# Windowed attention with split operands: the values' high and low halves in one 128-column stationary operand

## The chip, the cores and the metric

The kernel runs on one core of a Trainium2 chip, in float32 throughout. The metric is the device time of one launch in microseconds (us). The kernel before takes 1700.15 us, the median of three runs (1699.94, 1700.15 and 1702.44).

Engine names follow the profile: PE is TensorE's matmul stream and PEld its weight loads, which overlap it; DVE is VectorE, ACT is ScalarE, POOL is GpSimd, SP is the queue that issues most DMAs. PSUM is the accumulator memory into which PE writes.

## The reference

The reference is a two-layer transformer block for 512 tokens and 256 context tokens, width 1024. Layer 0 (even) mixes tokens by a gated MLP and a differential attention, layer 1 (odd) by a windowed attention with a sink; each layer ends with a SwiGLU feed-forward network (FFN) of hidden width 2816. Every matrix product must come out in float32 accuracy. The part that the change touches is the odd attention, cut to its core:

```python
def sink_attend(q, kvs, sink):            # 16 query heads, 4 key/value heads of 64
    for k, v, mask in kvs:                # a band of up to 3 blocks of 128 keys, and the 256 context keys
        s = einsum('bqhgd,bkhd->bhgqk', q, k) * ATTN_SCALE     # masked in the band
    p = softmax(concatenate(scores + [s_sink]))
    out = sum over kvs of einsum('bhgqk,bkhd->bqhgd', p, v)

def odd_mixer(...):
    q, k, v = split(h @ w_qkv, ...)       # rope on q and k
    o = lax.map(block, ...)               # 4 query blocks of 128
    y = o @ w_out
```

## The kernel before

**Arithmetic.** PE takes its operands in a rounded 32-bit format (fp32r). To keep float32 accuracy, a value is split in a high part (the rounded value, written by ACT) and a low part (the rest, a subtraction on DVE or POOL): `split` at L113 to L116 for activations, `unit` at L67 to L79 for weights. A product then takes three passes, high times high, high times low and low times high, which is the helper `mm3` at L95 to L101 (one line for each pass: L99, L100, L101).

**Layout.** Activations stand transposed, features on the 128 partitions and tokens along the free dimension. The order in which each engine meets its instructions is not written by hand: the code is recorded in program order, and a scheduler that estimates durations interleaves independent pieces; afterwards every engine runs its own list strictly in order. Tiles come from pools in which a tag has a fixed number of buffers; a new tile of a tag waits until its buffer's last reader is done. PSUM tags are `b` (three banks, `bank`, shown as `pb`), `f` (one bank, `fill`, `pf`) and `w` (two double banks, `wide`, `pw`).

**The odd attention** (`odd`, L1070 to L1241). Keys and values are projected first; the values of six blocks of 128 tokens are split by L115 and L116 into tiles `vhi` and `vlo` of 128 x 256 (four heads of 64). The work is then cut into two halves of 256 tokens and four key/value heads g; in `attend(g, half)` two query blocks i follow each other. One block does this:

1. `softmax`: for four query heads, scores by six or more matmuls into a `pw` bank (L1150, masks L1155, L1158), the row maximum (L1161) and a small minimum (L1162) on DVE, the exponential on ACT (L1164).
2. For each of the 4 or 5 key blocks kb (18 for the four query blocks, 72 in all): four transposes on PE into a bank `pt` (L1186), the split of that 128 x 512 tile (high on ACT, L115; low on DVE, L116), and `mm3` of the values with it into the block's accumulator `po`, the lower 64 partitions of a `b` bank. The stationary operand is `vhi` or `vlo` of one head, 128 x 64, the moving operand is 128 x 512.
3. Two ACT copies (L1194) bring the 64 x 512 accumulator to the output tile `raw`, whose partitions hold two heads each.
4. After two query blocks, four small transposes (L1201) and one DVE product (L1203) apply the softmax's denominators.

So `po`, `pt` and the bank of step 4 share the three `b` banks.

Other work is laid beside the attention: during the first half, the query projections of the next heads (`project_q`, into `pf`), and during the second half the output projection of the first half (`project(0, ...)`, 192 matmuls into `pf`), with its residual (L757), the squares of the new rows (L769 on ACT) and their sum (L773 on DVE). From that sum follow, still before the end of the attention, the reciprocal root (four matmuls L149 into `pf`, the small DVE steps L156 and L128 to L132, L165, and L175 on PE) and the FFN's modulated input of the first 256 tokens (L831 on DVE, L835 on ACT). After the attention comes the output projection of the second half (`project(1, ...)`, 192 matmuls into `pb`, whose weights' low parts are made on DVE, L78), then the same chain for the second 256 tokens, and the FFN.

The squares' tiles come from `tmp()` (L110): tag `q` of a pool that lives through the whole kernel, 128 x 512, two buffers, used in the program's order.

## Time and profile before

| what | value |
|---|---|
| median of three runs | 1700.15 us |
| profiled execution, its own time | 1697.54 us |
| its span on the chip | 1695.8 us |
| PE, DVE, ACT, POOL busy in the span | 92%, 68%, 44%, 48% |
| odd attention (first score matmul to last value matmul) | about 1039 to 1248 us of the span |
| output projection of the second half | 1247.9 to 1277.4 us |

The profiled execution lies 2.6 us under the median and 1.74 us over its own span. A busy share of PE counts each matmul from its start to the modelled end of its pipeline, so that neighbours overlap; the distance from one start to the next is what a matmul costs. In a list of groups, a row gives source line, engine, operation, output and input tiles, shapes, count, then busy time and mean duration, then idle time of the engine just before and what ended it. In a list of waits, a row says who waited for whom, how long in total, how often, and the longest. The chain of waits is followed back from the last instruction; the row "by line" gives the shares of a stretch.

### The profile page before, as it was taken

What the parts mean: (1) busy time and instruction counts of PE and PEld (TensorE: products, weight loads), DVE (VectorE), ACT (ScalarE), POOL (GpSimd) and SP (SyncE); (2) the same over time, 40 slices, a digit from 0 to 9 for tenths busy, and PEclk for the clock granted to TensorE, in tenths of its full rate; (3) what the DMA queues carried; (4) which work ended last, traced back from release to release, by engine and by line L of the source; (5) the groups of instructions that cost most, each with busy time, mean ns of one, the idle gap of its engine ahead of it and who ended that gap; (6) DMA issues with size and microseconds to landing.
All of it is one profiled execution on the core that took longest, in us unless ns stands there. A gap on an engine that the chain in (4) does not pass through costs nothing.

```text
span 1695.8 us, 24602 instructions
## 1 busy us (share of the span) xinstructions
PE 1558.7 (92%) x9415; PEld 1379.5 (81%) x9415; DVE 1145.4 (68%) x2037; ACT 752.8 (44%) x1521; POOL 806.8 (48%) x586
## 2 busy tenths in 40 slices
PE   6999989798899999999999988999987898999996
PEld 4776878698798889888899977778866788888986
DVE  4613788856967677666765676777769865756566
ACT  3413676433533233333333345676655444444443
POOL 0562211232675566656665336512115665666673
PEclk9999989899899899999999999999998999999998
DMA  8753100241032343344341112101140322222311
GB/s 312 290 184 133 32 1 1 87 159 41 25 125 88 124 136 110 127 136 135 132 132 38 49 63 75 51 7 45 50 146 10 125 90 98 87 100 78 110 38 50
DMA packets 47958, 161.98 MB, mean 96 GB/s; under 512 B 5472, under 2 KB 9952, under 8 KB 40160
## 3 DMA queue, kind: packets, MB, share of 16 engines
q1 hardware_dynamic: 47696, 160.28, 27.6%
q8 instruction: 74, 1.21, 0.3%
q14 instruction: 44, 0.36, 0.1%
q10 hardware_dynamic: 144, 0.13, 0.0%
HBM read 158.29 MB, written 2.10 MB: 95 GB/s over the span
## 4 chain that ended last, share of the span: by engine, by line
PE 65%; DVE 18%; DMA 6%; ACT 4%; issue 3%; POOL 3%; POOLq 0%; SPq 0%; DVEq 0%; ACTq 0%
PE pb L100 9%; PE pb L101 9%; PE pb L99 9%; PE pw L99 8%; PE pw L100 8%; PE pw L101 7%; DMA raw<-ffn_in 6%; POOL w L904 3%; DVE t L925 2%; PE pf L99 2%; PE pf L100 2%; PE pf L101 2%; PE pf L349 2%; DVE sq L925 1%; PE pb L1186 1%
## 5 line engine op out<-in xcount | busy, mean ns | idle before, releaser
L78 POOL TENSOR_TENSOR w<-raw,w 128x512 fp32r<-128x512 f32 (+1 forms) x84 | 128.6, 1540 | 234.3 <-ACT w L75 211.8
L99 PE MATMUL pw<-ax,w 128*128 128x384 f32 (+2 forms) x648 | 211.9, 331 | 18.0 <-DVE q L972 5.7
L904 POOL TENSOR_TENSOR w<-t,w 128x512 fp32r<-128x512 f32 x106 | 156.4, 1476 | 149.1 <-ACT w L901 146.0
L100 PE MATMUL pw<-ax,w 128*128 128x384 f32 (+2 forms) x648 | 210.7, 326 | 2.7 <-DVE ax L456 1.4
L101 PE MATMUL pw<-ax,w 128*128 128x384 f32 (+2 forms) x648 | 208.4, 324 | 3.1 <-DVE w L904 3.1
L757 DVE SCALAR_TENSOR_TENSOR xT<-pb,mod,xT 128x512 f32<-128x512 f32 (+3 forms) x208 | 143.9, 703 | 68.3 <-PE pb L101 67.9
L904 POOL TENSOR_TENSOR w<-raw,w 128x512 fp32r<-128x512 f32 x111 | 155.7, 1414 | 59.2 <-ACT w L901 59.2
L99 PE MATMUL pb<-hh,w 128*128 128x512 f32 x480 | 167.4, 363 | 14.8 <-ACT hh L115 7.9
L100 PE MATMUL pb<-hh,w 128*128 128x512 f32 x480 | 172.3, 361 | 0.7 <-POOL hh L116 0.2
L99 PE MATMUL pw<-T,w 128*128 128x384 f32 (+1 forms) x504 | 158.7, 318 | 12.2 <-DVE hs L968 9.5
L101 PE MATMUL pb<-hh,w 128*128 128x512 f32 x480 | 168.7, 359 | 0.0
L901 ACT CAST w<-t 128x512 fp32r<-128x512 f32 x120 | 74.2, 620 | 208.1 <-DVE t L925 176.8
L100 PE MATMUL pw<-T,w 128*128 128x384 f32 (+1 forms) x504 | 159.1, 316 | 7.0 <-DVE T L116 4.1
L101 PE MATMUL pw<-T,w 128*128 128x384 f32 (+1 forms) x504 | 158.3, 314 | 0.0
L99 PEld LDWEIGHTS pw<-ax,w 128*128 128x128 f32 x648 | 125.0, 194 | 32.8 <-DVE q L972 9.2
L100 PEld LDWEIGHTS pw<-ax,w 128*128 128x128 f32 x648 | 125.3, 193 | 10.5 <-DVE ax L193 3.3
L101 PEld LDWEIGHTS pw<-ax,w 128*128 128x128 f32 x648 | 124.8, 193 | 6.4 <-DVE w L904 3.3
L904 POOL TENSOR_TENSOR w<-rawo,w 128x512 fp32r<-128x512 f32 x74 | 107.2, 1448 | 39.1 <-ACT w L901 39.1
L99 PEld LDWEIGHTS pb<-hh,w 128*128 128x128 f32 x480 | 90.6, 191 | 28.5 <-ACT hh L115 9.0
L99 PEld LDWEIGHTS pw<-T,w 128*128 128x128 f32 x504 | 97.3, 194 | 18.9 <-DVE hs L968 11.9
L99 PE MATMUL pb<-ax,w 128*128 128x256 f32 (+1 forms) x344 | 106.8, 313 | 4.1 <-ACT w L75 2.2
L100 PE MATMUL pb<-ax,w 128*128 128x256 f32 (+1 forms) x344 | 106.3, 309 | 2.1 <-DVE ax L116 2.1
(381 smaller groups left out, 4324.4 us busy)
## 6 DMA issues: line engine op xcount, KB each, us to landing
raw<-ffn_in SPq DMA_DIRECT2D x44, 1024.0 KB, 5.7
ar<-ada SPq DMA_DIRECT2D x24, 1024.0 KB, 7.0
ar<-ada SPq DMA_DIRECT2D x48, 512.0 KB, 3.5
rawo<-ffn_out SPq DMA_DIRECT2D x44, 512.0 KB, 3.8
raw<-odd_out SPq DMA_DIRECT2D x32, 256.0 KB, 2.7
raw<-qk SPq DMA_DIRECT2D x16, 256.0 KB, 7.8
raw<-uv SPq DMA_DIRECT2D x16, 256.0 KB, 2.7
raw<-even_out SPq DMA_DIRECT2D x8, 512.0 KB, 3.5
```

What stands on the lines that cost most here:

```text
L78: eng.tensor_tensor(lo, raw, hi.bitcast(F32), ALU.subtract)
L99: mm(out, s[0], m[0], start=start, stop=False, **kw)
L100: mm(out, s[0], m[1], start=False, stop=False, **kw)
L101: mm(out, s[1], m[0], start=False, stop=stop, **kw)
L349: nc.tensor.matmul(ps[32 * q:32 * q + 32, :w], cst[:, k, :], t[:, w * q:w * q + w], start=k == 0, stop=k == KT - 1, skip_group_check=True)
L757: self.nc.vector.scalar_tensor_tensor(h, ps[:, r], self.modcol(l, j, m, who), h, ALU.mult, ALU.add)
L901: nc.scalar.copy(t[:, 0, :], src)
L904: eng.tensor_tensor(t[:, 1, :], src, t[:, 0, :].bitcast(F32), ALU.subtract)
L925: nc.vector.tensor_tensor(t, x, y, how)
L1186: nc.tensor.transpose(pt[:, x * P:(x + 1) * P], es[2 * (x % 2) + x // 2][:, kb * P:(kb + 1) * P], self.ident)
```

## The change

The values' high and low parts of one head become the two halves of one stationary operand of 128 columns. Against each of the two parts of the transposed probabilities it gives, in one pass, high values in the accumulator's partitions 0 to 63 and low values in partitions 64 to 127. So a key block takes two matmuls in place of three, and the product low times low, which was left out, is now in the sum. The accumulator `po` fills a whole bank. The two halves are joined at the end of each query block: ACT copies the half that lies in the other partitions to a `tmp()` tile (tag `q`), and DVE adds it to the half in PSUM into `raw`; two copies and two additions for each block, where two copies stood. The splits of the values and of the probabilities have the same number of instructions and elements; those of the values write runs of 64 elements into a tile that interleaves both parts by head.

```diff
-        vhi, vlo = [], []
+        V = []
...
         for tb in range(6):
-            hv, lv = [Rk.tile([P, TC], F32R, name=f"v1_{p}_{tb}") for p in range(2)]
-            self.split(hv, lv, acc[tb])
-            vhi.append(hv)
-            vlo.append(lv)
+            v = Rk.tile([P, 4, 2, 64], F32R, name=f"v1_{tb}")
+            self.split(v[:, :, 0, :], v[:, :, 1, :], acc[tb].rearrange("p (g d) -> p g d", d=64))
+            V.append(v.rearrange("p g c d -> p g (c d)"))
...
-                po = self.bank()[0:64, :]
+                po = self.bank()
...
-                    V = [v[vb][:, 64 * g:64 * g + 64] for v in (vhi, vlo)]
-                    self.mm3(po, V, (th, tl), kb == 0, kb == nb - 1)
+
+                    for p, t in enumerate((th, tl)):
+                        nc.tensor.matmul(po, V[vb][:, g, :], t, start=kb == 0 and p == 0, stop=kb == nb - 1 and p == 1)
+                c = slice(i % 2 * P, i % 2 * P + P)
+                o = raw[half, g]
                 pov = po.rearrange("p (h a q) -> p h a q", h=2, q=P)
+                lo = self.tmp()[:, :TC].rearrange("p (a q) -> p a q", q=P)
                 for par in range(2):
-                    nc.scalar.copy(raw[half, g][64 * par:64 * par + 64, :, i % 2 * P:i % 2 * P + P], pov[:, par, :, :])
+                    X = slice(64 * par, 64 * par + 64)
+                    nc.scalar.copy(lo[X], pov[64 - 64 * par:128 - 64 * par, par, :, :])
+                    nc.vector.tensor_tensor(o[X, :, c], pov[X, par, :, :], lo[X], ALU.add)
```

The scheduler sees other durations and other tiles and writes other lists. What differs beside the edits: the first half's seven sums of squares (L773), with the squares on ACT, the reciprocal root and the modulated input, which stood inside the attention, now stand after its last addition on DVE. On PE the projection of the second half is cut by them: 66 matmuls, the four L149, 30 matmuls, L175, 96 matmuls, where 192 stood in one piece. From the second L149 on, PE's list is the same as before.

## The prediction

> **What bounds the kernel now.** I read the page first, then busy time by stretch of the odd attention, then the chain of waits in each stretch. The page says that PE is the busiest engine; the span and PE's row:

> ```profile
> span 1695.8 us, 24602 instructions
> PE 1558.7 (92%) x9415; PEld 1379.5 (81%) x9415; DVE 1145.4 (68%) x2037; ACT 752.8 (44%) x1521; POOL 806.8 (48%) x586
> ```

> An average over stages says nothing about this one. Busy time in four stretches of the attention (columns: stretch, length, then PE, PEld, DVE, ACT, POOL busy with counts, granted clock, DMA share, GB/s):

> ```profile
> 1058.00:1098.00 40.00, 38.59 (x207) 31.24 (x208) 29.65 (x54) 23.01 (x49) 20.54 (x17) 1.00 0.17 53
> 1098.00:1158.00 60.00, 57.44 (x367) 45.24 (x365) 46.84 (x108) 43.94 (x108) 10.06 (x13) 1.00 0.03 10
> 1158.00:1208.00 50.00, 49.47 (x365) 44.69 (x366) 35.28 (x73) 34.22 (x83) 18.00 (x16) 1.00 0.23 69
> 1208.00:1248.00 40.00, 35.42 (x219) 26.17 (x219) 29.54 (x77) 25.24 (x61) 2.73 (x4) 1.00 0.19 67
> ```

> The first and the third have filling work on PE (query projections, then the output projection); the second and the fourth have nearly none. DVE is 74, 78, 71 and 74% busy. The value matmuls alone, in the same stretches (first pair after the length: PE busy and count):

> ```profile
> 1058.00:1098.00 40.00, 8.17 (x27) 3.51 (x27) 0.00 (x0) 0.00 (x0) 1.00 0.17 53
> 1098.00:1158.00 60.00, 26.98 (x81) 10.04 (x81) 0.00 (x0) 0.00 (x0) 1.00 0.03 10
> 1158.00:1208.00 50.00, 15.93 (x49) 6.20 (x49) 0.00 (x0) 0.00 (x0) 1.00 0.23 69
> 1208.00:1248.00 40.00, 20.02 (x59) 7.09 (x59) 0.00 (x0) 0.00 (x0) 1.00 0.19 67
> ```

> The chain of waits by line, one row for each stretch:

> ```profile
> by line: PE pf L99 14.6%; PE pf L101 13.2%; PE pf L100 13.1%; DVE sa L1161 6.0%; DVE sh L243 5.5%; DVE pt L116 5.0%; PE pb L1186 4.7%; DVE sa L1166 4.4%; DVE qf L244 4.3%; DVE sa L1162 3.9%; DVE qa L259 3.4%; PE pw L1150 3.3%; PE pw L1158 2
> by line: PE pb L1186 13.6%; PE pw L1150 12.7%; PE pb L100 9.2%; PE pw L1158 9.1%; PE pb L101 8.2%; DVE sa L1161 6.3%; PE pb L99 6.2%; ACT e L1164 6.0%; issue 5.0%; ACT pt L115 4.7%; DVE pt L116 4.5%; PE pw L1155 3.8%; ACT o L1194 3.7%; ACT
> by line: PE pb L1186 14.0%; PE pf L99 13.2%; PE pf L100 13.1%; PE pf L101 12.9%; PE pw L1150 9.1%; PE pb L100 7.8%; PE pw L1158 7.5%; PE pb L101 7.4%; PE pb L99 6.9%; PE pw L1155 3.2%; issue 1.5%; DVE pt L116 1.4%; ACT e L1164 1.1%; PE pb L
> by line: PE pb L1186 12.5%; PE pb L100 11.1%; DVE pt L116 10.2%; ACT pt L115 9.8%; PE pb L101 8.2%; ACT e L1164 7.2%; PE pw L1150 7.2%; PE pb L99 6.3%; PE pw L1158 5.8%; issue 3.8%; DVE sa L1161 3.5%; PE pw L1155 2.3%; DVE hm L831 1.9%; ACT
> ```

> In the third stretch the shares of PE shown add to 95%: PE is the limit there. In the second and fourth PE holds some 60%, and the rest goes round ACT and DVE: transposes, split on ACT, low part on DVE, matmul. Who waits for whom there:

> ```profile
> ACT pt L115 <- PE pb L1186: 28.6, 31, 2.6
> DVE pt L116 <- ACT pt L115: 21.4, 24, 3.1
> ACT o L1194 <- PE pb L101: 8.6, 9, 1.8
> PEld pb L100 <- DVE pt L116: 8.0, 16, 1.1
> PEld pb L99 <- ACT pt L115: 3.2, 6, 1.0
> ```

> **The change part by part.**

> *72 matmuls go.* What one costs is the distance between starts:

> ```profile
> 1133.22 0.40 PE L99 MATMUL pb<-pt,v 128*64 128x512 f32 x1
> 1133.45 0.39 PE L100 MATMUL pb<-pt,v 128*64 128x512 f32 x1
> 1133.68 0.39 PE L101 MATMUL pb<-pt,v 128*64 128x512 f32 x1
> 1133.91 0.27 PE L1186 MATMUL pb<-ident,e 128*128 128x128 f32 x1
> ```

> 0.23 us each, so 72 x 0.23 = 16.6 us of PE's list, one third of the counts above: 9, 27, 16 and 20 matmuls, or 2.1, 6.2, 3.7 and 4.6 us. What the chain gives of it: in the third stretch all of it, 3.7. In the second L101 holds 8.2% of 60 us = 4.9, in the fourth 8.2% of 40 = 3.3; there I count on a part, since DVE, which gets the additions, and the loop over ACT and DVE stand close behind: half of 4.9, 2.5, and 2.0 of 3.3. In the first stretch the rows of the query projection and its rope lead the chain and I take 1.0 of 2.1. Sum: 1.0 + 2.5 + 3.7 + 2.0 = 9.2 us. The ends: nothing but the third stretch (3.7), and everything that lies on the chain (2.1 + 4.9 + 3.7 + 3.3 = 14.0).

> *The remaining 144 have 128 columns of weights for 64.* Their nearest rows, a query projection of 128 columns and the old pass, differ little in matmul, more in weight load:

> ```profile
> L101 PE MATMUL pb<-pt,v 128*64 128x512 f32 x72 | 28.4, 395 | 0.0
> L101 PE MATMUL pf<-ax,w 128*128 128x512 f32 x49 | 19.2, 391 | 0.0
> L101 PEld LDWEIGHTS pb<-pt,v 128*64 128x64 f32 x72 | 9.7, 135 | 1.9
> L101 PEld LDWEIGHTS pf<-ax,w 128*128 128x128 f32 x112 | 21.1, 189 | 2.2
> ```

> A load of 189 ns hides under the 0.23 us of the matmul before it. Where a load waits itself (16 + 6 times in the list of waits) the 54 ns show: 22 x 0.054 = 1.2 us at most, 0.5 taken.

> *32 additions come on DVE, 64 x 256 from PSUM and SBUF.* Nearest rows: the low part of the values (128 x 256 out of PSUM), on ACT the copies of the same 64 x 256, which stay, and a subtraction of twice the length (weights' low parts, after the attention):

> ```profile
> L116 DVE TENSOR_TENSOR v<-pb,v x6: 411/414/424, 1023.2 to 1026.0; 128x256 fp32r<-128x256 f32 x6
> L1194 ACT COPY o<-pb x32: 352/366/368, 1077.9 to 1248.1; 64x256 f32<-64x256 f32 x32
> L78 DVE TENSOR_TENSOR w<-raw,w 128x512 fp32r<-128x512 f32 x11 | 7.2, 686 | 3.7 <-ACT w L75 3.6
> ```

> I take the 0.41 of the first row, which has as many elements along each partition: 32 x 0.41 = 13.1 us, ends 32 x 0.37 = 11.7 and 32 x 0.69 = 22.1. In the first and third stretch they lie beside PE's work. In the second they are 27 / 4.5 = 6 blocks x 0.82 = 4.9 us on a DVE that was busy for 46.8 of 60: that is why I left half of L101's chain time out there. In the fourth they are 4.4 x 0.82 = 3.6 us, and about as much leaves it (below).

> *po is held longer.* Its bank came free after two copies (0.73 us); now it waits for the second addition, and in DVE's new list a row maximum or a low part stands between the two additions of most blocks. At the 0.69 of a 128 x 512 subtraction that is 0.41 + 0.69 = 1.1 us later, 16 times, on one of three banks. The transposes of the next block's second key block wait for it. I cost it at nothing, because PE's list has one or two groups of score matmuls ahead of those transposes; without that cover it is 16 x 1.1 = 17.6 us, the first rival.

> *The copies on ACT, the splits of the values.* Same count and elements; nothing. Twelve splits with runs of 64 elements lie ahead of the first query projection, ends 0 and 12 x 0.2 = 2.4 us if each were half as long again.

> *The squares' chain moves behind the attention.* The new `tmp()` tiles are the last users of tag `q` in program order, so six of seven squares wait for the last additions. Behind them come the reciprocal root and the eight L831, into the projection of the second half. Its rows now, and what the later stage hangs on:

> ```profile
> 1247.86 0.36 PE L99 MATMUL pb<-ax,w 128*128 128x256 f32 x1
> 1261.02 0.41 PE L99 MATMUL pb<-ax,w 128*128 128x256 f32 x1
> 1261.23 0.41 PE L100 MATMUL pb<-ax,w 128*128 128x256 f32 x1
> 1276.88 0.28 PE L101 MATMUL pb<-ax,w 128*128 128x256 f32 x1
> 1277.00 0.28 PE L99 MATMUL pb<-ax,w 128*128 128x256 f32 x1
> 1277.36 0.60 PE L149 MATMUL pb<-ones,sq 128*128 128x128 f32 x4
> 1247.62 2.43 DVE L831 SCALAR_TENSOR_TENSOR hh<-xT,mod,pf 128x256 f32<-128x256 f32 x6
> L757 DVE SCALAR_TENSOR_TENSOR xT<-pb,mod,xT 128x256 f32<-128x256 f32 x6 | 2.9, 481 | 3.4 <-PE pb L101 3.4
> L773 DVE TENSOR_TENSOR sq<-sq,q 128x256 f32<-128x256 f32 x6 | 2.5, 420 | 1.6 <-ACT q L769 1.6
> by line: DVE t L925 18.8%; DVE ax L116 7.0%; DVE w L904 6.6%; DVE hh L873 6.0%; DVE sq L925 5.5%; DVE hm L873 5.0%; DVE sm L130 4.5%; DVE sm L131 4.5%; DVE hs L974 4.0%; DVE hh L831 3.4%; DVE hm L833 3.2%; DVE sm L132 2.6%; DVE T L116 2.3%;
> ```

> 192 matmuls at 0.12 are 23.0 us; they take 1277.36 - 1247.86 = 29.5, with 6.5 us of waits for weights and of slow matmuls. DVE is busy for 12.6 us of 1258 to 1278 (7.2 + 2.9 + 2.5), so there is room. In the new list: 66 matmuls, 7.9 us, in which DVE adds seven squares (2.9); L149, 0.5; 30 matmuls, 3.6, beside the root's small steps, which I take to be no longer than that; L175; then PE's last 96 wait for the ninth weight split, and ahead of it on DVE stand a residual, two sums, eight L831 and the split itself: 0.48 + 0.84 + 8 x 0.41 + 0.69 = 5.3 us idle; then 11.5. Sum 28.8, to which I add half of today's 6.5 of waits: 32.0, that is +2.5. Ends: -1.5 (what waits today is ready by then) and +6 (all 6.5 again). The last row says that DVE paces the start of the FFN, whose list is unchanged, so this goes through to the end.

> *Sum.* -9.2 + 0.5 + 2.5 = -6.2 us. Against the profiled execution's 1697.54 that is 1691.3; the median of the runs, 2.6 us above it, goes to 1693.9, say 1694.

> **The rivals.**

> *Slower: the accumulator's bank.* If PE has to wait for `po`'s second addition, the attention's blocks get longer by up to 1.1 us each. Two busy consumers speak for it: DVE, 78% busy in the second stretch, goes to (46.8 + 4.9) / 60 = 86% if the length stays. The cover by score matmuls speaks against it, and the old copies' wait, 8.6 us in 9 cases, was ACT's. It decides from 6.2 / 16 = 0.39 us a block; at 0.75 it is +12.0 - 6.2 = +5.8: 1706.

> *All of it.* If the loop over ACT and DVE has slack wherever L101 lay on the chain: -14.0 + 0.5 + 2.5 = -11.0: 1689. The third stretch's 95% speaks for it, the second's 60% against.

> *No change: the passes were not the limit.* If in the second and fourth stretch PE only waits longer for the loop over ACT and DVE (28.6 and 21.4 us of waits in the whole attention today), 3.7 + 1.0 is left, and with +4 at the joint it is 1700.15 - 0.7 = 1699.5.

> *A slower clock at the joint.* The matmuls at 1261.02 stand 0.21 apart, those at 1276.88 0.12: a stretch of PE at nearly half rate. One or two more such stretches of some 3.5 us, brought on by the 5.3 us in which PE would idle, cost 1.5 to 3 us, and give 1695.5 to 1697. [...] The two distances here, 0.21 and 0.12, agree with half against full.

> **How the numbers follow.** The sum as worked out 0.40 (own range 1690 to 1697), all of it 0.13, no change 0.13, the clock 0.08, the bank 0.26. About 0.2% (3.4 us) is what a measurement of this kernel can tell from no change. Faster: 0.40 + 0.13 = 0.53; same: 0.13 + 0.08 = 0.21; slower 0.26. The range takes the upper half of "all of it" and the lower half of the slower case: 1686 to 1706.

> **What would show it.** Right: 144 value matmuls with starts 0.23 apart; the stretch from the first score matmul to the last value matmul, 1039 to 1248 now, some 9 us shorter; 32 additions of about 0.4; one idle gap of 4 to 5 us in PE after L175; the second L149 some 32 us after the projection's first matmul. Wrong: waits of transposes (L1185 in the new numbering) for the additions (L1199), or DVE over 85% busy in the second stretch at the old length. The sum falls if the FFN's part, whose list is the same, moves by more than 2 us.

## The result, and the profile after

The changed kernel takes 1706.36 us (median of 5 executions, 1702.07 to 1709.53), the kernel before in its five 1700.15 (1699.74 to 1702.44): a ratio of 1.0038 with a 95% interval of 1.0022 to 1.0054. It is slower, by 6.5 us. 1694 was forecast, and the median lies 0.4 us above the range of 1686 to 1706.

The profiled execution took 1705.45 us. The page's span and engines (busy us, share, instructions):

```profile
span 1703.7 us, 24513 instructions
PE 1551.6 (91%) x9343; PEld 1375.5 (81%) x9343; DVE 1151.5 (68%) x2069; ACT 754.6 (44%) x1521; POOL 809.3 (48%) x586
```

72 matmuls are gone and PE is busy for 7.1 us less than before; the program is longer all the same. The same four stretches of the attention as in the prediction, all engines, then the value matmuls alone in the second and the third:

```profile
1058.00:1098.00 40.00, 38.01 (x205) 31.69 (x205) 30.79 (x58) 23.61 (x50) 21.36 (x18) 1.00 0.17 53
1098.00:1158.00 60.00, 50.68 (x311) 41.53 (x311) 48.25 (x111) 41.01 (x99) 9.19 (x12) 0.97 0.03 10
1158.00:1208.00 50.00, 46.88 (x348) 43.20 (x347) 34.01 (x72) 31.75 (x73) 16.90 (x15) 1.00 0.23 74
1208.00:1248.00 40.00, 33.73 (x202) 25.45 (x201) 31.53 (x76) 27.64 (x67) 2.92 (x4) 1.00 0.16 61
```

```profile
1098.00:1158.00 60.00, 20.73 (x52) 9.28 (x52) 0.97 0.03 10
1158.00:1208.00 50.00, 12.03 (x31) 5.26 (x29) 1.00 0.23 74
```

PE, at 57.4 of 60 us before, now stands at 50.7 in the second stretch: it idles for 9.3 us there. DVE went from 46.8 to 48.3, 80% of the stretch: no engine is full. Who waits for whom, from the first query projection to the last value matmul (waiting engine, tile and line, released by; us, times, longest):

```profile
PEld pb L1191 <- DVE pt L116: 15.1, 24, 1.6
PE pb L1191 <- DVE pt L116: 7.6, 18, 1.4
DVE o L1199 <- ACT q L1198: 4.0, 6, 1.4
PEld pb L1185 <- DVE o L1208: 2.8, 3, 1.2
PE pb L1185 <- DVE o L1208: 2.0, 3, 0.9
PE pb L1185 <- DVE o L1199: 0.3, 1, 0.3
PEld pb L1185 <- DVE o L1199: 0.3, 2, 0.2
```

The same view of the kernel before:

```profile
PEld pb L100 <- DVE pt L116: 8.0, 16, 1.1
PE pb L100 <- DVE pt L116: 2.5, 8, 0.9
PEld pb L1186 <- DVE o L1203: 0.4, 1, 0.4
```

The value pass that uses the low parts of the transposed probabilities (L116 on DVE) waits for them about twice as long as before: 22.7 us in its two rows together, 10.5 before. (The rows of PEld and of PE overlap in time, so such a sum counts waits and isn't lost time.) New are the waits of the transposes (L1185) for the product L1208, which comes after the last addition of a pair of blocks and holds a bank that they need. The waits for the additions themselves, which the first rival forecast, are 0.6 us.

Where the 7.9 us between the two profiled executions arose, in sections cut at PE's rows (start of the first query projection; last value matmul; second L149; end): -0.1 ahead of the attention, +3.6 in it (223.3 to 226.9), +2.8 at the joint (30.1 to 32.9), +1.5 in the FFN (418.4 to 419.9).

**Half-rate stretches.** Before these numbers are compared further, one thing has to be taken out of them. The first query projections of the kernel before, and of a kernel whose list is the same there (*x5_layout* below), one row for each matmul (start, us, engine, line; in brackets the idle time before it):

```profile
1032.12 0.47 PE L99 MATMUL pf<-ax,w 128*128 128x512 f32 x1 [2.49 <-DVE qf L244]
...
1033.56 0.63 PE L101 MATMUL pf<-ax,w 128*128 128x512 f32 x1
1033.98 0.63 PE L99 MATMUL pf<-ax,w 128*128 128x512 f32 x1
```

```profile
1035.09 0.47 PE L99 MATMUL pf<-ax,w 128*128 128x512 f32 x1 [2.49 <-DVE qf L244]
...
1036.32 0.39 PE L101 MATMUL pf<-ax,w 128*128 128x512 f32 x1
1036.55 0.40 PE L99 MATMUL pf<-ax,w 128*128 128x512 f32 x1
```

PE stood still for the same 2.49 us in both. Then the matmuls stand 0.42 us apart in one execution for some 3.4 us (granted clock 0.50 from 1033.1 to 1036.5 us), and 0.23 apart in the other (clock 1.00). That execution of the kernel before finishes its first block 2.5 us later (52.3 against 49.8 us from the projection's start), and from there on all blocks take the same time to 0.2 us. The attention of the changed kernel holds two such stretches, this one and another of 3.4 us around 1133:

```profile
1127.80:1131.20 3.40, 2.50 (x16) 1.79 (x14) 3.31 (x6) 1.33 (x3) 1.29 (x1) 1.00 0.14 40
1131.20:1134.60 3.40, 2.67 (x8) 2.01 (x9) 1.12 (x2) 2.66 (x7) 0.00 (x0) 0.62 0.10 37
```

A kernel with nearly the same order of work (*e2_own_tag*) has no such stretch at that place, and the block there is 1.3 us shorter. So below, next to the time, stands the length of the attention with such stretches taken out: 2.3 us for the one at the first projections (the difference of the two attentions above, 223.3 and 221.0), 1.3 for each further one. The first is measured on equal lists, the further ones cost 1.0 to 1.5 (*x6_prio* below); carried over to other kernels both are estimates.

### The profile page after: what moved, and what is told of

It is laid out like the page before. It is cut to its first block, busy times and chain, and to the rows that moved or that the text cites. A ratio compares the mean times of both kernels' runs of the same rounds, so it can differ in the third digit from the quotient of the medians.

```text
span 1703.7 us, 24513 instructions
## 1 busy us (share of the span) xinstructions
PE 1551.6 (91%) x9343; PEld 1375.5 (81%) x9343; DVE 1151.5 (68%) x2069; ACT 754.6 (44%) x1521; POOL 809.3 (48%) x586
## 4 chain that ended last, share of the span: by engine, by line
PE 58%; DVE 20%; DMA 7%; POOL 6%; issue 5%; ACT 5%; POOLq 0%; SPq 0%; DVEq 0%; ACTq 0%
PE pb L99 7%; PE pb L100 7%; PE pw L99 7%; PE pb L101 7%; PE pw L100 7%; PE pw L101 7%; DMA raw<-ffn_in 6%; POOL w L904 4%; DVE t L925 3%; PE pf L99 2%; PE pf L100 2%; PE pf L101 2%; PE pf L349 2%; DVE junk L220 1%; PE pb L1191 1%
## 5 line engine op out<-in xcount | busy, mean ns | idle before, releaser
L78 POOL TENSOR_TENSOR w<-raw,w 128x512 fp32r<-128x512 f32 (+1 forms) x84 | 127.4, 1525 | 229.4 <-ACT w L75 203.8
L904 POOL TENSOR_TENSOR w<-t,w 128x512 fp32r<-128x512 f32 x106 | 155.1, 1464 | 153.2 <-ACT w L901 150.0
L99 PE MATMUL pw<-ax,w 128*128 128x384 f32 (+2 forms) x648 | 211.9, 331 | 16.8 <-DVE hs L977 4.6
L100 PE MATMUL pw<-ax,w 128*128 128x384 f32 (+2 forms) x648 | 211.2, 326 | 2.7 <-DVE ax L456 1.4
L101 PE MATMUL pw<-ax,w 128*128 128x384 f32 (+2 forms) x648 | 208.6, 325 | 3.1 <-DVE w L904 3.1
L757 DVE SCALAR_TENSOR_TENSOR xT<-pb,mod,xT 128x512 f32<-128x512 f32 (+3 forms) x208 | 144.2, 704 | 62.4 <-PE pb L101 61.7
L99 PE MATMUL pb<-hh,w 128*128 128x512 f32 x480 | 166.7, 362 | 14.8 <-ACT hh L115 7.9
L904 POOL TENSOR_TENSOR w<-raw,w 128x512 fp32r<-128x512 f32 x111 | 155.8, 1416 | 45.7 <-ACT w L901 45.4
L100 PE MATMUL pb<-hh,w 128*128 128x512 f32 x480 | 172.1, 360 | 1.6 <-POOL hh L116 1.0
L101 PE MATMUL pb<-hh,w 128*128 128x512 f32 x480 | 168.6, 359 | 0.0
L100 PE MATMUL pw<-T,w 128*128 128x384 f32 (+1 forms) x504 | 157.8, 313 | 11.3 <-POOL T L116 6.7
L99 PE MATMUL pw<-T,w 128*128 128x384 f32 (+1 forms) x504 | 157.5, 316 | 9.6 <-DVE hs L968 7.2
L101 PE MATMUL pw<-T,w 128*128 128x384 f32 (+1 forms) x504 | 156.9, 312 | 0.0
L99 PEld LDWEIGHTS pw<-ax,w 128*128 128x128 f32 x648 | 124.9, 193 | 30.9 <-DVE q L972 7.6
L100 PEld LDWEIGHTS pw<-ax,w 128*128 128x128 f32 x648 | 125.5, 194 | 10.5 <-DVE ax L193 3.2
L101 PEld LDWEIGHTS pw<-ax,w 128*128 128x128 f32 x648 | 125.2, 194 | 6.4 <-DVE w L904 3.3
L904 POOL TENSOR_TENSOR w<-rawo,w 128x512 fp32r<-128x512 f32 x74 | 107.3, 1450 | 37.5 <-ACT w L901 37.5
L99 PEld LDWEIGHTS pb<-hh,w 128*128 128x128 f32 x480 | 90.2, 190 | 28.5 <-ACT hh L115 9.0
L99 PE MATMUL pb<-ax,w 128*128 128x256 f32 (+1 forms) x344 | 107.5, 315 | 6.1 <-ACT w L75 3.4
L100 PEld LDWEIGHTS pw<-T,w 128*128 128x128 f32 x504 | 96.5, 191 | 16.0 <-POOL T L116 7.5
L99 PEld LDWEIGHTS pw<-T,w 128*128 128x128 f32 x504 | 96.1, 192 | 16.2 <-DVE hs L968 9.1
```

The costliest lines, as they stand in the source:

```text
L78: eng.tensor_tensor(lo, raw, hi.bitcast(F32), ALU.subtract)
L99: mm(out, s[0], m[0], start=start, stop=False, **kw)
L100: mm(out, s[0], m[1], start=False, stop=False, **kw)
L101: mm(out, s[1], m[0], start=False, stop=stop, **kw)
L757: self.nc.vector.scalar_tensor_tensor(h, ps[:, r], self.modcol(l, j, m, who), h, ALU.mult, ALU.add)
L904: eng.tensor_tensor(t[:, 1, :], src, t[:, 0, :].bitcast(F32), ALU.subtract)
```

## The experiments

All ran beside the kernel before. "At full rate" is the corrected length of the attention, from the first query projection to the last value matmul.

| kernel | median us | ratio to before, 95% | attention in the trace | half-rate stretches of 3.4 us in it | at full rate |
|---|---|---|---|---|---|
| before | 1700.15 | | 223.3 | 1 | 221.0 |
| the change | 1706.36 | 1.0038 [1.0022, 1.0054] | 226.9 | 2 | 223.3 |
| e1_no_join | 1694.58 | 0.9979 [0.9965, 0.9993] | 214.4 | 0 | 214.4 |
| e2_own_tag | 1704.82 | 1.0041 [1.0023, 1.0059] | 227.2 | 1 | 224.9 |
| e3_three_and_join | 1716.49 | 1.0094 [1.0076, 1.0112] | 239.7 | 3 | 234.8 |
| e4_third_pass | 1712.89 | 1.0081 [1.0066, 1.0097] | 238.9 | 1 | 236.6 |
| e6_act_pool | 1704.61 | 1.0026 [1.0010, 1.0041] | 225.0 | 2 | 221.4 |
| e7_act_pool_once | 1727.75 | 1.0166 [1.0147, 1.0184] | 248.2 | 7 | |
| e8_hold | 1698.81 | 1.0006 [0.9988, 1.0024] | 222.8 | 1 | 220.5 |
| e9_load | 1699.11 | 1.0002 [0.9988, 1.0016] | 224.9 | 3 | 220.0 |
| x3_before_no_clamp | 1699.41 | 1.0012 [0.9997, 1.0027] | 223.5 | 0 | 223.5 |
| x4_own_tag_no_clamp | 1700.54 | 1.0015 [1.0002, 1.0027] | 223.3 | 1 | 221.0 |
| x5_layout | 1700.56 | 1.0002 [0.9991, 1.0013] | 221.0 | 0 | 221.0 |
| x6_prio | 1709.49 | 1.0061 [1.0045, 1.0078] | 229.8 | 3 | 224.9 |
| y6_load_early | 1696.96 | 0.9990 [0.9976, 1.0004] | 217.7 | 0 | 217.7 |

**The passes without the join.**

```diff
-                    nc.scalar.copy(lo[X], pov[64 - 64 * par:128 - 64 * par, par, :, :])
-                    nc.vector.tensor_tensor(o[X, :, c], pov[X, par, :, :], lo[X], ALU.add)
+                    nc.scalar.copy(o[X, :, c], pov[0:64, par, :, :])
```

> Two passes with 128 columns as in the change, but the join is left out: two ACT copies bring the high half alone to the output tile, as before, with no addition and no temporary tile, so the product of the values' low parts is left out of the result. If the join (additions on DVE and the accumulator's bank held for them) is what took the gain, the attention gets 9 us shorter than before (1039 to about 1239) and the time is about 1691. If the passes were never the limit, the attention stays within 3 us of the 208.3 us from first score matmul to last value matmul and the time is 1697 to 1700. The squares' chain is back inside the attention in both cases.

The attention is 6.6 us shorter than before at full rate (221.0 to 214.4; 8.9 in the traces as they are), and the time falls by a ratio of 0.9979, 3.6 us. Leaving out a third of the value matmuls does help, by less than the 9.2 us forecast.

**The change with a buffer of its own for the low half.**

```diff
-                lo = self.tmp()[:, :TC].rearrange("p (a q) -> p a q", q=P)
+                lo = Rs.tile([P, TC], F32, name=self.uid("lo"), tag="lo", bufs=1).rearrange("p (a q) -> p a q", q=P)
```

> The change, with the join's temporary tile under a tag of its own (one buffer of 128 x 256), so that the squares of the first half need not wait for the last additions. If the moved chain at the joint is its whole price, the projection of the second half goes from 32 us back to 29.5 and the time is about 3 us under the changed kernel: 1703. The attention should stay some 4 us longer than before (theory of the join) or change by a scheduler's list that is different again.

The joint goes from 32.9 back to 30.6 us: the ring of tag `q` was what it cost. The time doesn't show it (1.0041 against 1.0038), because the attention is 1.6 us longer at full rate. With the join the attention takes 224.9 and without it 214.4: the join costs 10.5 us here, 8.9 in the change as it is (223.3).

**Three passes and the join; a third pass on the change.** The first is the kernel before with its two copies replaced by a copy and an addition of the same half (the output is doubled), the second is *e2_own_tag* with

```diff
-                    for p, t in enumerate((th, tl)):
+                    for p, t in enumerate((th, tl, th)):
```

and `stop` at the third pass, so that the probabilities' high parts count twice.

> The kernel before, three passes with 64 columns, plus a join of the same size under a tag of its own: two copies to a temporary tile and two additions on DVE of 64 x 256 in place of two copies, so the result is doubled. If the join takes what the passes give (additions and bank cost some 10 us or more), the time is 1709 or more. If the additions are free and the passes are free too, it stays at 1700 to 1702.

> The changed kernel with the tag of its own and a third pass of 128 columns (the high part of the probabilities once more, so the result is wrong by that term). If passes are the limit in part of the attention, it is slower than the kernel with the tag of its own by up to 16.6 us, and by at least the 3.7 us of the filled stretch. If the loop over ACT and DVE hides them, it is within 3 us of it.

The join on top of three passes costs 16 us by the ratio, and some 14 in the attention at full rate (221.0 to 234.8; 16.4 in the traces as they are). A third pass costs 11.7 in the attention at full rate (224.9 to 236.6), of 16.6 us of matmuls. The join isn't a small price that the removed pass uncovered: three passes hide it no better.

**Who could carry the join instead.** ACT copies both halves, four copies a block, and POOL adds in SBUF; then the same with one POOL addition for two blocks:

```diff
-                    nc.vector.tensor_tensor(o[X, :, c], pov[X, par, :, :], lo[X], ALU.add)
+                    nc.scalar.copy(o[X, :, c], pov[X, par, :, :])
+                    nc.gpsimd.tensor_tensor(o[X, :, c], o[X, :, c], lo[X], ALU.add)
```

> The change with the join moved off DVE: ACT copies both halves (four copies of 64 x 256 a block in place of two), and POOL, some 30% busy here, adds them in SBUF; tag of its own. DVE has no join at all and the bank is free after four copies on ACT. If DVE's time or its queue in front of the bank is the cause, the stretch comes to 214 to 221 us (32 more copies of 0.37 on an ACT that is 65% busy cost part of the gain) and the time is under the kernel before. If any longer evacuation of the accumulator costs as much, it stays at 227.

> As the one with four copies on ACT and the addition on POOL, but one addition of 128 x 512 for two query blocks, from a tile of the probabilities' ring, in place of four of 64 x 256: less POOL time, a tile of the ring held longer. Within 3 us of the other if POOL is not in the way; slower by more if the ring of six tiles is.

The first was expected under the time of the kernel before, and is nearly as slow as the change (1.0026). Its waits for the low parts are nearly as short as without a join:

```profile
PEld pb L1191 <- DVE pt L116: 9.3, 20, 0.8
PE pb L1191 <- DVE pt L116: 3.2, 12, 0.6
PEld pb L1185 <- DVE o L1209: 0.8, 1, 0.8
```

but ACT, busy for 153 us in place of 142, has 30 more copies to make in that stretch, and the attention is still 7.0 us longer than without a join (221.4 against 214.4). The second, with its low halves in the ring of the probabilities' parts, is far slower; I didn't take its cause apart.

**The hold of the bank and the load on DVE, one without the other.** Both start from *e1_no_join*. *e8_hold*: behind each copy a DVE operation on two columns that reads the bank and waits for the copy, as the addition does. *e9_load*: behind each copy a DVE operation of the addition's size that works on the output tile and leaves the bank alone.

```diff
+                    h = o[X, 0, c.start:c.start + 2]
+                    nc.vector.tensor_tensor(h, pov[0:64, par, 0, 0:2], h, ALU.max)
```

```diff
+                    nc.vector.tensor_tensor(o[X, :, c], o[X, :, c], o[X, :, c], ALU.max)
```

> The kernel without the join (two passes, high half alone copied; the product of the values' low parts is left out), and behind each copy a DVE instruction that reads two columns of the accumulator and leaves the result as it is: the bank is held until DVE has come to it, at hardly any DVE time. If the held bank is what the join costs, first query projection to last value matmul goes from 214.4 us without the join back towards the changed kernel's 227.0, and the time is some 9 us over the kernel without the join. If it is DVE's time, it stays within 4 us of 214.4.

> The kernel without the join (the product of the values' low parts is left out), and behind each copy a DVE instruction of the join's size, 64 x 256, on the output tile alone, which leaves it as it is: DVE has the join's time, and the accumulator's bank comes free after the copies. If DVE's time is what the join costs, the same stretch goes from 214.4 us to about 227; if it is the held bank, it stays within 4 us of 214.4.

Neither reaches the join's price; each costs about half of it: 6.1 us for the hold (214.4 to 220.5), 5.6 for the load (to 220.0). From the end of a block's last value matmul to the last read of its accumulator, the mean of the 16 blocks is 2.75 us in *e8_hold*, 0.99 in *e9_load* and 0.93 without a join. Their groups (count, busy us, mean ns of one, idle time before them), within the attention, *e8_hold* first:

```profile
L1199 DVE TENSOR_TENSOR o<-pb,o 64x2 f32<-64x2 f32 x30 | 4.4, 148 | 6.5 <-ACT o L1197 6.3
```

```profile
L1198 DVE TENSOR_TENSOR o<-o 64x256 f32<-64x256 f32 x30 | 14.4, 480 | 1.1 <-ACT o L1197 0.6
```

The tiny operations are busy for 4.4 us, but DVE stands for 6.5 more because they are next in its list and the copy isn't done. In both kernels the value matmuls then wait for the low parts as in the change. *e8_hold*:

```profile
PEld pb L1191 <- DVE pt L116: 15.6, 27, 1.7
PE pb L1191 <- DVE pt L116: 7.5, 16, 1.5
PE pb L1185 <- DVE o L1199: 0.5, 1, 0.5
```

The held bank makes PE wait for 0.5 us in this row; the late low parts make up 23.1 in the two rows above it. *e8_hold* has both the longer hold and DVE standing before a copy, so it doesn't say which of the two makes the low parts late.

**DVE time taken out elsewhere.** The softmax's minimum with the sink (64 operations, 18.8 us) leaves the kernel before, and *e2_own_tag*; the line is L1162 in the one and L1161 in the other:

```diff
-                nc.vector.tensor_tensor(c, c, nsink[:, 4 * g + x:4 * g + x + 1], ALU.min)
```

> The kernel before without one small VectorE instruction of each head's softmax: the exponent's shift is the row maximum alone, not its minimum with the sink's. 64 instructions of 64 x ~295 ns = 18.8 us leave VectorE; the ratio that is computed is mathematically the same. Theory (every microsecond on VectorE in the attention's loop lengthens it, by 0.6 to 0.75): first query projection to last value matmul 8 to 14 us shorter than the 223.3 of before, time 1686 to 1692. Rival (VectorE has slack at 70 to 78% and only where and behind what the join stands matters): within 3 us of before.

> The change with a buffer of its own for the join's low half, and without the same 64 small instructions. Theory (the join costs by VectorE's time): 18.8 us leave and 12.6 had come, so the attention falls from 227 to 213 to 219, and the time to 1690 to 1697. Rival (the join costs by the hold of the bank or by its place in VectorE's queue): attention 224 to 228, time 1701 to 1706.

Busy time of the attention, *e1_no_join*, *x4_own_tag_no_clamp* and *x3_before_no_clamp* (length; PE, PEld, DVE, ACT, POOL; clock):

```profile
1031.90:1246.30 214.40, 195.30 (x1203) 164.01 (x1201) 161.63 (x341) 141.56 (x327) 72.61 (x65) 1.00 0.16 52
```

```profile
1024.00:1247.30 223.30, 199.67 (x1203) 165.93 (x1201) 161.20 (x307) 145.13 (x327) 72.94 (x65) 0.99 0.15 50
```

```profile
1025.80:1249.30 223.50, 207.39 (x1275) 167.65 (x1274) 151.05 (x277) 143.31 (x327) 72.61 (x65) 1.00 0.15 50
```

*x4_own_tag_no_clamp* was the run that told most. With the join and without the minimum, DVE is as busy as in the kernel without a join (161.2 and 161.6 us), and the attention is still 6.6 us longer at full rate (221.0 against 214.4). And 10.7 us less on DVE than before (161.75 to 151.05) makes the kernel before no faster. My theory, that every microsecond on DVE counts, expected 1686 to 1692 from *x3_before_no_clamp* and fell with 1699.41. The amount isn't the cause, or not most of it. It has some part: the 221.0 of *x4_own_tag_no_clamp* lies under the 224 to 228 that the rival had expected, and 3.9 us under *e2_own_tag*, for 18.8 us of operations taken out.

**The layout alone, and the join's place by priority.** *x5_layout* is the kernel before with the values' parts side by side. *x6_prio* is *e2_own_tag* with the join under a raised priority.

```diff
-                    V = [v[vb][:, 64 * g:64 * g + 64] for v in (vhi, vlo)]
-                    self.mm3(po, V, (th, tl), kb == 0, kb == nb - 1)
+                    self.mm3(po, (V[vb][:, g, 0:64], V[vb][:, g, 64:128]), (th, tl), kb == 0, kb == nb - 1)
```

```diff
+                with tc.high_priority(offset=40):
                     for par in range(2):
```

> The kernel before with the changed layout of the values alone: high and low parts of a head group side by side, three passes of 64 columns and the two old copies. Both theories: the same as before, attention 221 to 226 us, time within 3 us. If it is slower by more, part of the change's loss is the splits' layout and not the join.

> The change with a buffer of its own for the low half and the join's copies and additions put ahead in the order of their engines' lists. Theory (VectorE's time): the same attention as without, 225 to 229 us. Rival (the bank is held too long, the additions come too late in VectorE's list): attention 218 to 223, time 1694 to 1699.

The layout costs nothing (1.0002). The priority moved no instruction in any engine's list, so *x6_prio* tells nothing on the place. Its time, 1.0061 against 1.0041, shows how far two measurements of the same lists lie apart here, 3.4 us. It is of use as a second execution of *e2_own_tag*'s order: 14 of 16 blocks take the same time to 0.1 us, two are 1.5 and 1.0 us longer, and each of these holds a half-rate stretch that the other trace lacks.

**The same load in another place.** *e1_no_join* with 32 DVE operations of 64 x 256 on a scratch tile that nobody waits for, two in each softmax:

```diff
                 nc.vector.tensor_tensor(c, c, nsink[:, 4 * g + x:4 * g + x + 1], ALU.min)
+                if par == 0:
+                    nc.vector.scalar_tensor_tensor(zz[0:64], zz[0:64], c[0:64], zz[0:64], ALU.mult, ALU.add)
```

> Two passes, the high half copied alone, no join, and 32 VectorE operations on 64x256 of a scratch tile that nothing waits for, two in each block's softmax, right behind a row maximum: as much work as the join's additions, in another place of VectorE's list and with no wait for a copy. Compared at equal clock with the two passes alone (first query projection to last value matmul 214.4) and with the same load behind the copies (some 219 to 220). Theory (place: what costs is work and waits in VectorE's list just ahead of the low parts of the weights, for which the second value pass waits): attention 213 to 217, sum of the value matmuls' waits for the low parts near 10 us. Rival (amount: 13 to 14 us more on VectorE cost the same wherever they stand): attention 219 to 223, those waits near 20 us.

Their group, the attention's busy times, and the value matmuls' waits:

```profile
L1166 DVE SCALAR_TENSOR_TENSOR zz<-zz,sa 64x256 f32<-64x256 f32 x32 | 18.5, 579 | 0.4
```

```profile
1026.40:1244.10 217.70, 196.34 (x1203) 163.95 (x1201) 176.39 (x373) 142.31 (x327) 72.73 (x66) 1.00 0.16 52
```

```profile
PEld pb L1196 <- DVE pt L116: 12.6, 22, 1.5
PE pb L1196 <- DVE pt L116: 6.2, 13, 1.3
```

18.5 us on DVE, more than the join's 12.6 in the same section of *e2_own_tag*, cost 3.3 us (214.4 to 217.7), where the join costs 10.5. By these, 12.6 us of mere DVE time would cost 12.6 x 3.3 / 18.5 = 2.2 us, an estimate with which the 3.9 us for 18.8 of *x4_own_tag_no_clamp* agree. The attention lies between the two expectations, 0.7 us above what the theory of the place allowed and 1.3 below the rival's least; the sum of the two waits, 18.8 us, is where the rival had put it. So those waits count how often PE finds a low part late, but don't measure what it costs: *x4_own_tag_no_clamp* has 29.6 us of them in an attention of 221.0. The amount is the smaller part of the join's price.

That the rest is the place, and the wait that goes with it, is argued and not shown, because one rival is left: the order of everything else. Each kernel is scheduled anew. With the value matmuls left out, PE has 1058 matmuls in the attention of *e1_no_join*, and to get the list of another kernel one has to move at least 58 of them for *y6_load_early*, 88 for *e9_load*, 122 for *e8_hold* and 141 for *e2_own_tag*. Their prices rise in the same order: 3.3, 5.6, 6.1 and 10.5 us. From the kernel before to *x3_before_no_clamp* it is 153, and that attention is 2.5 us longer with less work. No run here has the join in the lists of a kernel without it.

## Why the prediction was wrong

**The step that failed is "32 additions come on DVE": they have no term in the sum.** In the first and third stretch they were to "lie beside PE's work"; in the second they only halved the gain taken from L101, and in the fourth as much other work was to leave DVE. The duration was right: 0.41 us forecast, and all 32 of the change:

```profile
L1199 DVE TENSOR_TENSOR o<-pb,q 64x256 f32<-64x256 f32 x32 | 13.4, 419 | 5.4 <-ACT q L1198 4.9
```

But with their copies and the lists that come with them they cost 8.9 us in the attention (214.4 without, 223.3 with), and 10.5 in *e2_own_tag*. A busy share of 70 to 80% was read as room. The additions stand at the end of a block in DVE's list, and the list is worked in order; a block's value accumulation ends, ACT copies, DVE adds, and behind it wait the next blocks' row maxima and low parts. The runs show pieces of the price: DVE time as such (some 2 us by *y6_load_early*); the hold of the bank together with the time for which DVE stands before a copy that isn't done (*e8_hold* costs 6.1 us with tiny operations); and the product L1208, which now comes after the second addition and keeps its bank (4.8 us of waits of transposes, 0.4 before). They overlap, each comes with another order of the lists, and I can't give each an exact share: that the join costs this much is shown, by which of these it does so stays open. In the third stretch, where PE's shares of the chain add to 95%, the additions weren't beside PE's work either: from the ninth to the eleventh block *e2_own_tag* is 4.0 us longer than *e1_no_join* (15.3 + 13.7 + 19.1 against 13.4 + 10.3 + 20.4).

**"72 matmuls go", -9.2: right in kind, too large by 2.6 us.** At full rate it is -6.6, within the ends of 3.7 and 14.0. The trace of before, from which the -9.2 was worked out, held a half-rate stretch that *e1_no_join*'s lacks; without the correction the two traces differ by 8.9, which would have looked like a perfect forecast.

**"The remaining 144 have 128 columns of weights for 64", +0.5:** their loads take 189 ns, as forecast, and no run tells their price apart.

**"po is held longer", at nothing: the wait of the transposes was right, the hold was not.** Transposes wait 0.6 us for the additions. But the bank was to come free 1.1 us later, and from the end of a block's last value matmul to its last read it is 2.99 us on the mean of the 16 blocks, 0.88 before. The join is a chain across two engines: both copies write one tile, and in all 16 blocks the second copy starts only after the first addition has read it. One block (start, us):

```profile
1216.32 0.37 ACT L1198 COPY q<-pb 64x256 f32<-64x256 f32 x1 [1.17 <-PE pb L1191]
1216.83 0.41 DVE L1199 TENSOR_TENSOR o<-pb,q 64x256 f32<-64x256 f32 x1
1217.27 0.36 ACT L1198 COPY q<-pb 64x256 f32<-64x256 f32 x1 [0.58 <-DVE o L1199]
1217.67 0.43 DVE L1199 TENSOR_TENSOR o<-pb,q 64x256 f32<-64x256 f32 x1 [0.36 <-ACT q L1198]
```

What the join costs with a tile for each half, no run here tells. The first rival's 1706 is the time that came, but not as it was worked out, so the hit is luck: PE itself waits 0.6 us for the bank, and what its rows show late is the low parts on DVE. Whether the longer hold helps to make them late, the runs don't part. DVE over 85% in the second stretch, the other sign named for this case, didn't come either: it is 80%.

**"The copies on ACT, the splits of the values", nothing:** right for the splits (*x5_layout*, 1.0002). The copies take as long as before (368 ns for 366), but ACT now stands 2.8 us before them for the additions.

**"The squares' chain moves behind the attention", +2.5: right.** PE idles behind L175, in the end for the reason forecast, the split L78 behind eight L831 on DVE; the first 2.98 us end with ACT's L75, which itself had waited 1.13 us for the weights' transfer:

```profile
1251.56 0.36 PE L99 MATMUL pb<-ax,w 128*128 128x256 f32 x1
...
1263.69 0.67 PE L175 MATMUL pf<-q,ones 128*128 128x256 f32 x2
1267.34 0.39 PE L99 MATMUL pb<-ax,w 128*128 128x256 f32 x1 [2.98 <-ACT w L75]
1267.57 0.28 PE L100 MATMUL pb<-ax,w 128*128 128x256 f32 x1
1268.73 0.58 PE L101 MATMUL pb<-ax,w 128*128 128x256 f32 x1 [0.88 <-DVE w L78]
1269.11 0.41 PE L99 MATMUL pb<-ax,w 128*128 128x256 f32 x1
```

2.98 + 0.88 = 3.9 us where 4 to 5 were named, and from the first projection matmul to the second L149 (1283.77) it is 32.2 us for a forecast of 32.0 and 29.5 before. With the buffer of its own it goes away.

**"A slower clock at the joint":** the matmuls behind the gap do stand 0.21 apart, for one stretch (granted clock 0.50 from 1268.6 to 1272.0 us), as they did before (1258.4 to 1261.8); there is no further one. One more did come, but its place was the attention, where the changed kernel's profiled execution has it from 1132.0 to 1135.5. The order of work doesn't bring it on by itself: *e2_own_tag* hasn't got it.

**The sum.** Forecast: -9.2 + 0 + 0.5 + 2.5 = -6.2. Measured in the profiled execution: -6.6 for the passes, +8.9 for the join, +1.3 for one half-rate stretch more in the attention, +2.8 at the joint, +1.5 and -0.1 for the rest: +7.8, of the 7.9 between the two executions. Without the half-rate stretch and the rest it would be +5.1, inside the interval of the times (0.0022 to 0.0054, 3.7 to 9.2 us).

Two things stay open. The time of *e1_no_join* falls by 3.6 us (1.2 to 6.0) where its attention is 6.6 shorter at full rate, and all kernels with two passes are 1 to 4 us slower in the median than their attention says (*x6_prio* 6.5); more half-rate stretches in an emptier PE would do that (the mean clock of the twelve executions of *e1_no_join* is 0.9703, of the 18 of the kernel before beside them 0.9721, by estimate two stretches more), but I haven't shown it. And *x3_before_no_clamp*, with 64 DVE operations fewer than before, has an attention 2.5 us longer; its lists are ordered differently, and why that loses I don't know. The change's lists differ from those before by more than the squares' chain, too: some 120 of those 1058 matmuls of the attention are moved, and the sum has no term for that. No kernel here that computes the reference is faster than the one before beyond its interval.

## What to carry to other kernels

An operation that is added at the end of a loop's step, on an engine that works its list in order and has the next step's input behind it, isn't hidden by that engine's idle share: price it by its place, its own wait included, and ask what stands behind it and how often the new chain changes engines. Test such a price with two kernels, the same work in a place that nobody waits behind, and a tiny operation with the same wait, and count first how far a new order of the lists sets each of them apart. And before 1 or 2 us of a single trace are explained, look whether both traces had the same clock at that place.

## What the runs showed of the hardware that I had not expected

Behind much the same idle gap in PE at the first projections (2.5 us; 2.95 in *e6_act_pool*), 3.4 us at half rate follow in one execution and none in another: of the fifteen traces, eleven have the stretch at that place and four don't (*e1_no_join*, *x3_before_no_clamp*, *x5_layout*, *y6_load_early*). The granted clock of an execution, 0.966 to 0.975 on the mean, adds up to some 25 to 35 such stretches by estimate (the lost share of the span over the 1.7 us that one loses); those in the attention cost 1.0 to 2.5 us each. A stretch begins behind gaps of under 1 us too: in the change, at 1132.0, where the gaps just ahead are 0.84 and 0.73 us:

```profile
1130.20 0.50 PE L1191 MATMUL pb<-pt,v 128*128 128x512 f32 x1 [0.84 <-DVE pt L116]
...
1131.87 1.52 PE L1191 MATMUL pb<-pt,v 128*128 128x512 f32 x2 [0.73 <-ACT pt L115]
```

```profile
1029.70:1033.10 3.40, 0.98 (x4) 0.86 (x5) 2.24 (x4) 0.65 (x2) 3.19 (x3) 1.00 0.10 19
1033.10:1036.50 3.40, 3.40 (x9) 2.65 (x8) 0.26 (x1) 0.90 (x2) 2.37 (x2) 0.50 0.46 135
```

```profile
1033.30:1036.70 3.40, 1.61 (x7) 1.38 (x8) 1.61 (x4) 0.02 (x1) 3.40 (x3) 1.00 0.23 71
1036.70:1040.10 3.40, 3.40 (x17) 2.79 (x16) 0.82 (x2) 1.47 (x3) 1.77 (x2) 1.00 0.31 83
```

PE is busy for 24 to 44% of that piece in the eleven traces with the stretch, for 45 to 52% in the four without, by estimate from rows of 2 and 4 us (the stretches of the other thirteen lie at such marks too, to 0.06 us). The gap begins 0.05 us ahead of a mark in the kernel before and 0.7 us ahead of one in *x5_layout*, and the lists of these two kernels are the same: where the marks fall differs between these two executions.

No gap of PE in the attention is as long as a piece, 2.49 us at most in the kernel before and 2.50 in the change, and half rate followed the first row above with PE busy for 0.98 of its 3.40 us. Over the twelve executions of *e1_no_join* a mean clock lower by 0.001 goes with 0.9 us more, and a straight line through them explains some 40% of the scatter of 10 us between its times (1690.11 to 1700.38).
